# Half of each MLP down product as seven products for eight, woven with the next up chunk

## The chip, the cores and the metric

The kernel runs on one core of one Trainium2 chip. The metric is the time of one execution on the device in microseconds (us), as the median of three runs. A profile is one further execution, recorded by the hardware profiler; its span is shorter than a run's time by what lies around the program.

## The reference

A decoder trunk of two layers over 256 tokens of 2048 channels, all in float32. Each layer adds a mixer (layer 0: attention and pooling, layer 1: a gated convolution) and then an MLP whose hidden width is 8192. The change concerns the MLP:

```python
def _mlp(h, w_up, w_down):
    return jnp.square(jax.nn.relu(h @ w_up)) @ w_down

for layer in range(DEPTH):                      # DEPTH = 2
    h = _rmsnorm(x, mix_norm_g[layer])
    ...                                         # x = x + mixer(h)
    x = x + _mlp(_rmsnorm(x, mlp_norm_g[layer]), w_mlp_up[layer], w_mlp_down[layer])
```

x is 256 x 2048, an up weight 2048 x 8192, a down weight 8192 x 2048.

## The kernel before

**Precision.** Every float32 operand of a matmul is held as two parts in a rounded float32 format: hi, the leading twelve bits of each element (a cast on ScalarE, ACT, L124), and lo, the rest (a subtraction on VectorE, DVE, L125). A product is hi x hi + hi x lo + lo x hi. `slab` (L110) loads 1 MB of a weight into a raw buffer over the sync engine's queue and makes from it two pairs of hi and lo tiles, each 128 partitions x 1024 elements. There are three raw buffers, and six hi and six lo tiles.

**Up.** The hidden width is cut into 16 chunks of 512 columns. `up_chunk(c)` goes through `columns_chunk` (L153): four slabs, each with four blocks of 128 input channels (kt). For each kt and each of four column tiles, `columns_out` issues a matmul of 512 columns with the weight's hi (L144: the activations' hi and lo side by side) and one of 256 columns with its lo (L145). The results stand transposed (hidden columns in the partitions, tokens in the free axis) in two PSUM tiles of two banks each. There are four such tiles (`bank2`). `sum_halves` then adds the two halves of a result (ACT copies one to t, L171; DVE adds, L173), DVE makes relu squared in one instruction (L693), and `split` writes hi (ACT, L177) and lo (DVE, L178) into hT, which later serves as the stationary operand.

**Down.** A pair is two chunks, 1024 rows of the down weight. `down_block(pair, b)` makes 512 of the 2048 output columns for both blocks of 128 tokens: 2 slabs x 4 rows' tiles x 2 token blocks x 3 matmuls = 48 matmuls of 512 columns (`tokens_out`, L137, L138, L139), summed up in two PSUM banks. Two DVE instructions (L717) then scale these by the norm's 1/r^2 of each token and add them onto x.

**Order.** The loop at the end of `mlp` makes chunks 0 and 1 of a layer first. Then, for each of eight pairs, come an up chunk of the next pair, down blocks 0 and 1, the other up chunk, and down blocks 2 and 3. A half round is one up chunk and two down blocks, a round two of these. The program is written as one sequence. The framework's scheduler gives each engine its own sequence from it, with semaphores where an operand or a buffer has to be waited for. An engine works strictly in the order of its own sequence, and loads are issued by the sync engine (SP) in the same way, each when its raw buffer comes free.

## Time and profile before

| | before |
|---|---|
| time, median of 3 runs | 2065.22 us (2065.14 to 2070.14) |
| span of the profiled execution | 2063.8 us |
| matmuls that load a weight's lo or hi, up: L144 and L145 | 2816 each |
| matmuls for tokens: L137, L138, L139 | 1344 each |
| MB read from HBM | 380.39 |

Engines are PE (TensorE's matmuls), PEld (its weight loads, beside the matmuls), DVE (VectorE), ACT (ScalarE), POOL (GpSimd) and SP (SyncE). A row of a group reads: line, engine, operation, output <- inputs (partitions x elements), count | busy time, mean ns of one | idle time of the engine ahead of them, and what ended it. A row of a timeline starts with the start and the length in us and ends with the idle time ahead of it in brackets, if any. A row of the waits reads: the waiting instruction <- what released it: us, count, longest. The chain that ended last is followed back from the last instruction to what released each one. Of PE the recorded length of a matmul (0.39 us) overlaps the next one's, so its pace is read from the starts.

### The profile page before, as it was taken

What the parts mean: (1) busy time and instruction counts of PE and PEld (TensorE: products, weight loads), DVE (VectorE), ACT (ScalarE), POOL (GpSimd) and SP (SyncE); (2) the same over time, 40 slices, a digit from 0 to 9 for tenths busy, and PEclk for the clock granted to TensorE, in tenths of its full rate; (3) what the DMA queues carried; (4) which work ended last, traced back from release to release, by engine and by line L of the source; (5) the groups of instructions that cost most, each with busy time, mean ns of one, the idle gap of its engine ahead of it and who ended that gap; (6) DMA issues with size and microseconds to landing.
All of it is one profiled execution on the core that took longest, in us unless ns stands there. A gap on an engine that the chain in (4) does not pass through costs nothing.

```text
span 2063.8 us, 26221 instructions
## 1 busy us (share of the span) xinstructions
PE 2050.2 (99%) x10702; PEld 1751.5 (85%) x10702; DVE 1237.2 (60%) x1445; ACT 947.7 (46%) x1204; POOL 52.5 (3%) x76
## 2 busy tenths in 40 slices
PE   8999999999999999999999999999999999999999
PEld 7988888888888888888888888888888888888887
DVE  5677566555555555566666666556556555555554
ACT  5576554444444444444444444444444444444442
POOL 2330000000000000000000000000000000000000
PEclk9999999999999999999999999999999999999999
DMA  7553555555555555555555555555555555555553
GB/s 261 163 198 130 163 180 188 185 196 190 184 187 192 192 184 188 193 190 184 184 184 193 195 184 190 182 190 193 184 190 191 190 185 189 197 185 184 190 195 125
DMA packets 195817, 384.18 MB, mean 186 GB/s; under 512 B 6224, under 2 KB 16336, under 8 KB 195696
## 3 DMA queue, kind: packets, MB, share of 16 engines
q1 hardware_dynamic: 195312, 382.23, 56.5%
q8 instruction: 83, 1.36, 0.3%
q0 software_dynamic: 352, 0.27, 0.1%
q14 instruction: 38, 0.31, 0.0%
q10 hardware_dynamic: 32, 0.01, 0.0%
HBM read 380.39 MB, written 2.10 MB: 185 GB/s over the span
## 4 chain that ended last, share of the span: by engine, by line
PE 98%; DMA 1%; ACT 1%; SPq 0%; DVE 0%; issue 0%
PE ps L144 32%; PE ps L145 16%; PE ps L139 16%; PE ps L138 15%; PE ps L137 15%; PE ps L150 1%; PE ps L151 1%; PE ps L152 1%; PE ps L268 1%; DMA raw<-in_even_w_in 1%; PE ps L586 0%; PE ps L590 0%; ACT hi L124 0%; PE ps L578 0%; PE ps L622 0%; ACT junk L479 0%
## 5 line engine op out<-in xcount | busy, mean ns | idle before, releaser
L125 DVE TENSOR_TENSOR lo<-raw,hi 128x1024 fp32r<-128x1024 f32 (+2 forms) x722 | 884.3, 1226 | 704.9 <-ACT hi L124 704.0
L124 ACT CAST hi<-raw 128x1024 fp32r<-128x1024 f32 (+2 forms) x722 | 756.3, 1049 | 958.2 <-PE ps L144 497.1
L144 PE MATMUL ps<-xT,hi 128*128 128x512 f32 x2816 | 988.1, 396 | 0.0
L145 PE MATMUL ps<-xT,lo 128*128 128x256 f32 x2816 | 786.5, 279 | 0.0
L144 PEld LDWEIGHTS ps<-xT,hi 128*128 128x128 f32 x2816 | 528.5, 188 | 126.8
L145 PEld LDWEIGHTS ps<-xT,lo 128*128 128x128 f32 x2816 | 530.7, 188 | 1.2
L139 PE MATMUL ps<-hi,hT 128*128 128x512 f32 (+1 forms) x1344 | 526.7, 392 | 0.0
L137 PE MATMUL ps<-hi,hT 128*128 128x512 f32 (+1 forms) x1344 | 524.2, 390 | 0.0
L138 PE MATMUL ps<-lo,hT 128*128 128x512 f32 (+1 forms) x1344 | 523.7, 390 | 0.0
L138 PEld LDWEIGHTS ps<-lo,hT 128*128 128x128 f32 x1344 | 252.4, 188 | 55.2
L137 PEld LDWEIGHTS ps<-hi,hT 128*128 128x128 f32 x1344 | 252.4, 188 | 55.1 <-issue 1.3
L139 PEld LDWEIGHTS ps<-hi,hT 128*128 128x128 f32 x1344 | 252.5, 188 | 52.5
L717 DVE SCALAR_TENSOR_TENSOR x<-ps,r,x 128x512 f32<-128x512 f32 x129 | 90.5, 742 | 36.2 <-PE ps L139 36.1
L171 ACT COPY t<-ps 128x512 f32<-128x512 f32 x88 | 51.2, 582 | 50.9 <-PE ps L145 50.9
L173 DVE TENSOR_TENSOR h<-ps,t 128x512 f32<-128x512 f32 x64 | 43.9, 687 | 16.9 <-ACT t L171 16.9
L177 ACT CAST hT<-sq 128x512 fp32r<-128x512 f32 x64 | 39.8, 622 | 16.0 <-DVE sq L693 16.0
L693 DVE SCALAR_TENSOR_TENSOR sq<-h 128x512 f32<-128x512 f32 x64 | 44.3, 692 | 2.1
L178 DVE TENSOR_TENSOR hT<-sq,hT 128x512 fp32r<-128x512 f32 x64 | 43.8, 684 | 0.0
L181 ACT ACTIVATE xT<-ps,gains 128x256 fp32r<-128x256 f32 x64 | 30.1, 470 | 28.9 <-DVE xT L182 25.3
L137 PE MATMUL ps<-hi,xT 128*128 128x384 f32 (+1 forms) x96 | 32.8, 343 | 5.5 <-ACT hi L124 3.0
L182 DVE SCALAR_TENSOR_TENSOR xT<-ps,gains,xT 128x256 fp32r<-128x256 f32 x64 | 30.7, 480 | 12.4 <-ACT xT L181 12.2
L150 PE MATMUL ps<-xT,hi 128*128 128x256 f32 x128 | 36.4, 284 | 0.0
(157 smaller groups left out, 679.0 us busy)
## 6 DMA issues: line engine op xcount, KB each, us to landing
raw<-in_w_mlp_up SPq DMA_DIRECT2D x128, 1024.0 KB, 5.2
raw<-in_w_mlp_down SPq DMA_DIRECT2D x128, 1024.0 KB, 5.0
raw<-in_odd_w_in SPq DMA_DIRECT2D x48, 1024.0 KB, 5.1
raw<-in_even_w_out SPq DMA_DIRECT2D x16, 1024.0 KB, 5.1
raw<-in_odd_w_out SPq DMA_DIRECT2D x16, 1024.0 KB, 5.0
raw<-in_even_w_in SPq DMA_DIRECT2D x8, 1024.0 KB, 5.4
raw<-in_even_w_in SPq DMA_DIRECT2D x7, 1088.0 KB, 6.6
raw<-in_even_w_ukv SPq DMA_DIRECT2D x4, 1024.0 KB, 5.2
```

The source lines that it names most:

```text
L124: a = nc.scalar.copy(h, r)
L125: v = nc.vector.tensor_tensor(out=l, in0=r, in1=h.bitcast(F32), op=ALU.subtract)
L137: nc.tensor.matmul(o, lhsT=a_hi, rhs=hi[:, c0:c0 + n], start=first, stop=False)
L138: nc.tensor.matmul(o, lhsT=a_hi, rhs=lo[:, c0:c0 + n], start=False, stop=False)
L139: nc.tensor.matmul(o, lhsT=a_lo, rhs=hi[:, c0:c0 + n], start=False, stop=last)
L144: nc.tensor.matmul(o, lhsT=hi[:, c0:c0 + P], rhs=act[:, kt, :], start=first, stop=False)
L145: nc.tensor.matmul(o[:, S:2 * S], lhsT=lo[:, c0:c0 + P], rhs=act[:, kt, 0:S], start=False, stop=last)
L150: nc.tensor.matmul(o, lhsT=hi[:, c0:c0 + P], rhs=act[:, kt, 0:S], start=first, stop=False)
L171: nc.scalar.copy(t, ps[:, :, S:2 * S])
L173: nc.vector.tensor_tensor(out=u, in0=ps[:, :, 0:S], in1=t, op=ALU.add)
L693: nc.vector.scalar_tensor_tensor(out=sq, in0=u, scalar=0.0, in1=u, op0=ALU.max, op1=ALU.mult)
L717: nc.vector.scalar_tensor_tensor(out=xb, in0=ps[:, t, :n], scalar=r2[0][:, t:t + 1], in1=xb, op0=ALU.mult, op1=ALU.add)
```

## The change

For all pairs but the last of each layer, output columns 0 to 1023 (down blocks 0 and 1) are computed by `down_seven`. It takes the product as 2 x 2 x 2 blocks: two token blocks, even and odd tiles of rows, and two blocks of 512 columns. Instead of eight block products (96 matmuls in all) it makes seven, P1 to P7, of 12 matmuls each (L764 to L766), by an identity of the Strassen family. Some of the seven take sums of blocks as operands. Sums of weight blocks are made in place on DVE, four a pair of 128 x 2048 elements (L783, L786), ahead of the cut into hi and lo. Sums of the activations' blocks are made in `sum_forms` (L744, L745, L746, and a cut into hi and lo), behind each up result. The seven results are combined by further sums (L783), partly from copies that ACT keeps in SBUF (L779), and go onto x by L790.

The seven products are woven with up chunk 2p+2: P1, slab 0, P2, slab 1, P3, slab 2, P4, slab 3, P5, then that chunk's tail (its sums, relu, square and forms) together with P6 and P7. Then come up chunk 2p+3 and down blocks 2 and 3 as before. Relu squared is now two ACT instructions (L728, L730) in all chunks. The pools of raw buffers and halves are opened anew by `new_stage` for each stage of the program: two raw buffers in the MLP stage instead of three, with three block buffers of the same size beside them, and a place is waited for tile by tile. The last pair is computed as before.

The bodies of `slab` and `columns_chunk` are cut in two: `halved` makes hi and lo of a raw tile (casts at L140, subtractions at L141), and `columns_steps` stops behind each slab. The lines move: L144 and L145 are L160 and L161 now, L137 to L139 are L153 to L155, L171 and L173 are L194 and L196, L177 and L178 are L200 and L201, L717 is L850.

```diff
-    raws = ctx.enter_context(tc.tile_pool(name="raws", bufs=3))
-    halves = ctx.enter_context(tc.tile_pool(name="halves", bufs=6))
+    def new_stage(raw_bufs, **more):
+        for s_ in stage:
+            s_.close()
+        st = ExitStack()
+        stage[:] = [st]
+        pools.clear()
+        for name, bufs in dict(raws=raw_bufs, halves=6, **more).items():
+            pools[name] = st.enter_context(tc.tile_pool(name=uid(name), bufs=bufs, reuse_waits="tile"))
...
     def mlp(layer, ss, xT, after=None):
...
+        new_stage(2, blocks=3, forms=2)
+        pairs = DFF // NB // 2
         def up_chunk(c):
+            pss = []
+            yield from columns_steps(pss, up, xT, c * NB, 4)
             hT = act_tile()
-            for i, ps in enumerate(columns_chunk(up, xT, c * NB, 4)):
+            seven = c < 2 * (pairs - 1)
+            if seven:
+                fT = pools["forms"].tile([P, 2, 2, 4, P], F32R, tag="fT", name=uid("fT"))
+            for i, ps in enumerate(pss):
                 u = sum_halves(ps, "h")
+                nc.scalar.activation(u, u, AF.Relu)
                 sq = small.tile([P, 2, S], F32, tag="sq", name=uid("sq"))
-                nc.vector.scalar_tensor_tensor(out=sq, in0=u, scalar=0.0, in1=u, op0=ALU.max, op1=ALU.mult)
+                nc.scalar.activation(sq, u, AF.Square)
                 split(hT[:, 2 * i:2 * i + 2, 0:S], hT[:, 2 * i:2 * i + 2, S:2 * S], sq)
+                if seven:
+                    sum_forms(fT[:, i], sq.rearrange("p e (t s) -> p (e t) s", t=T))
...
+        def sum_forms(fT, a):
+            f = small.tile([P, 4, P], F32, tag="u", name=uid("f"))
+            nc.vector.tensor_tensor(out=f[:, 0:2, :], in0=a[:, 1:2, :].to_broadcast([P, 2, P]), in1=a[:, 0:4:3, :], op=ALU.subtract)
+            nc.vector.tensor_tensor(out=f[:, 2, :], in0=a[:, 3, :], in1=f[:, 0, :], op=ALU.subtract)
+            nc.vector.tensor_tensor(out=f[:, 3, :], in0=a[:, 2, :], in1=f[:, 2, :], op=ALU.subtract)
+            split(fT[:, 0], fT[:, 1], f)
+        def down_seven(pair):
...
+            def product(o, b, left):
+                for q, (hi, lo) in enumerate(halved(b)):
+                    a_hi, a_lo = left(2 * pair + q // 2, q % 2)
+                    nc.tensor.matmul(o, lhsT=a_hi, rhs=hi, start=q == 0, stop=False)
+                    nc.tensor.matmul(o, lhsT=a_hi, rhs=lo, start=False, stop=False)
+                    nc.tensor.matmul(o, lhsT=a_lo, rhs=hi, start=False, stop=q == 3)
...
+            yield
+            b11 = block(0, 0)
+            one = bank2()
+            product(one[:, 0, :], b11, own(0, 0))
+            s1 = kept(one[:, 0, :])
+            yield
+            b12 = block(0, 1)
+            minus(b11, b12, b11)
+            product(one[:, 1, :], b11, form(1))
+            s5 = kept(one[:, 1, :])
+            onto(0, 0, s1)
+            yield
+            b22 = block(1, 1)
+            two = bank2()
+            product(two[:, 0, :], b22, form(3))
+            onto(0, 1, two[:, 0, :])
+            yield
+            plus(b12, b22, b12)
+            plus(b22, b22, b11)
+            product(two[:, 1, :], b22, form(2))
+            plus(s1, two[:, 1, :], s1)
+            yield
+            three = bank2()
+            product(three[:, 0, :], b12, form(0))
+            e = pools["forms"].tile([P, NB], F32, tag="part", name=uid("part"), bufs=3)
+            plus(e, three[:, 0, :], s1)
+            onto(1, 0, e)
+            plus(s1, s1, s5)
+            onto(0, 1, s1)
+            plus(s5, e, s5)
+            onto(1, 1, s5)
+            yield
+            b21 = block(1, 0)
+            product(three[:, 1, :], b21, own(0, 1))
+            onto(0, 0, three[:, 1, :])
+            yield
+            minus(b22, b21, b22)
+            four = bank2()
+            product(four[:, 0, :], b22, own(1, 1))
+            onto(1, 0, four[:, 0, :])
...
+        for p in range(pairs - 1):
+            products, slabs = down_seven(p), up_chunk(2 * p + 2)
+            next(products)
+            for at in range(5):
+                next(products)
+                if at < 4:
+                    next(slabs)
+            whole(slabs)
+            whole(products)
+            whole(up_chunk(2 * p + 3))
+            for b in (2, 3):
+                down_block(p, b, False)
+        for b in range(4):
+            down_block(pairs - 1, b, True)
```

The first place is DVE's sequence where a half round ends and the next up chunk begins. Before the change (raw1004 is the first slab of that up chunk, ps979 and ps990 are the results of the two down blocks ahead of it):

```order
L125 TENSOR_TENSOR lo1000_6348<-raw996_6341,hi999_6347 128x1024
L125 TENSOR_TENSOR lo1006_6383<-raw1004_6380,hi1005_6382 128x1024
L717 SCALAR_TENSOR_TENSOR x_76<-ps979_6235,r2459_2894,x_76 128x512 x2
L125 TENSOR_TENSOR lo1008_6387<-raw1004_6380,hi1007_6386 128x1024
L125 TENSOR_TENSOR lo1011_6425<-raw1009_6422,hi1010_6424 128x1024
L125 TENSOR_TENSOR lo1013_6429<-raw1009_6422,hi1012_6428 128x1024
L125 TENSOR_TENSOR lo1016_6467<-raw1014_6464,hi1015_6466 128x1024
L717 SCALAR_TENSOR_TENSOR x_76<-ps990_6306,r2459_2894,x_76 128x512 x2
```

The first lo of the up chunk, lo1006, stands ahead of the additions onto x of both down blocks.

With the change DVE has, between the product P5 and the up chunk that follows P6 and P7 (the first bank of ps1175 is P5's, the second P6's, ps1196 is P7's; part tiles are the kept results, f the sums of activations, raw1203 the up chunk's first slab):

```order
L141 TENSOR_TENSOR lo1200_7087<-b1155_6866,hi1199_7086 128x1024
L744 TENSOR_TENSOR f1186_7036<-sq1185_7032 128x256
L783 TENSOR_TENSOR part1180_7018<-ps1175_6997,part1136_6752 128x512
L745 TENSOR_TENSOR f1186_7036<-sq1185_7032,f1186_7036 128x128
L790 SCALAR_TENSOR_TENSOR x_79<-part1180_7018,r2470_2931,x_79 128x512
L783 TENSOR_TENSOR part1136_6752<-part1136_6752,part1149_6821 128x512
L201 TENSOR_TENSOR hT1181_7025<-sq1185_7032,hT1181_7025 128x2x256
L790 SCALAR_TENSOR_TENSOR x_79<-part1136_6752,r2470_2931,x_79 128x512
L783 TENSOR_TENSOR part1149_6821<-part1180_7018,part1149_6821 128x512
L746 TENSOR_TENSOR f1186_7036<-sq1185_7032,f1186_7036 128x128
```

These are the last lo of P7, the sums that follow P5, and the forms of the up chunk's first result. They are followed without a gap by:

```order
L790 SCALAR_TENSOR_TENSOR x_79<-part1149_6821,r2470_2931,x_79 128x512
L196 TENSOR_TENSOR h1188_7044<-ps1138_6755,t1187_7042 128x512
L201 TENSOR_TENSOR fT1182_7026<-f1186_7036,fT1182_7026 128x512
L790 SCALAR_TENSOR_TENSOR x_79<-ps1175_6997,r2470_2931,x_79 128x512
L790 SCALAR_TENSOR_TENSOR x_79<-ps1196_7081,r2470_2931,x_79 128x512
L201 TENSOR_TENSOR hT1181_7025<-sq1189_7047,hT1181_7025 128x2x256
L744 TENSOR_TENSOR f1190_7051<-sq1189_7047 128x256
L141 TENSOR_TENSOR lo1205_7108<-raw1203_7105,hi1204_7107 128x1024
L745 TENSOR_TENSOR f1190_7051<-sq1189_7047,f1190_7051 128x128
L141 TENSOR_TENSOR lo1207_7112<-raw1203_7105,hi1206_7111 128x1024
```

The first lo of the next up chunk, lo1205, now stands behind all additions onto x of the seven products and behind most of the tail of the chunk before.

The second place is the same boundary in PE's sequence. Before, the last matmuls of a down block and the first of the up chunk:

```order
L137 MATMUL ps990_6306<-hi999_6347,hT848_5390 128x512
L138 MATMUL ps990_6306<-lo1000_6348,hT848_5390 128x512
L139 MATMUL ps990_6306<-hi999_6347,hT848_5390 128x512
L144 MATMUL ps1002_6378<-xT370_2325,hi1005_6382 128x512
L145 MATMUL ps1002_6378<-xT370_2325,lo1006_6383 128x256
```

The second matmul of the up chunk is the first to take its lo. With the change, from the last matmuls of P7:

```order
L764 MATMUL ps1196_7081<-hi1199_7086,hT1098_6555 128x512
L765 MATMUL ps1196_7081<-lo1200_7087,hT1098_6555 128x512
L766 MATMUL ps1196_7081<-hi1199_7086,hT1098_6555 128x512
L160 MATMUL ps1201_7103<-xT374_2333,hi1204_7107 128x512
L160 MATMUL ps1202_7104<-xT374_2333,hi1204_7107 128x512
L161 MATMUL ps1201_7103<-xT374_2333,lo1205_7108 128x256
```

The scheduler has put two matmuls with hi (one for each of the two results) ahead of the first with lo; the three rows above them end the seven products.

## The prediction

> **What bounds the kernel now.** I read the page first, then the waits of PE, then the rounds of the MLP in the timelines.

> ```profile
> span 2063.8 us, 26221 instructions
> PE 2050.2 (99%) x10702; PEld 1751.5 (85%) x10702; DVE 1237.2 (60%) x1445; ACT 947.7 (46%) x1204; POOL 52.5 (3%) x76
> PE 98%; DMA 1%; ACT 1%; SPq 0%; DVE 0%; issue 0%
> ```

> The chain that ended last is PE for 98%. PE's waits show where it was ever held:

> ```profile
> PE ps L209 <- DMA rows<-in_mix_norm_g: 3.4, 1, 3.4
> PE ps L137 <- ACT hi L124: 3.0, 1, 3.0
> PE ps L137 <- ACT xT L181: 2.6, 1, 2.6
> ```

> These are the three longest, all in the first 20 us; in the MLP there are none. So the kernel is as long as its matmuls: a matmul removed counts in full, as long as PE gets no new wait. A stretch of the MLP shows what is spare on the other engines (the columns are PE, PEld, DVE, ACT, POOL busy, then the clock):

> ```profile
> 500.00:582.00 82.00, 82.00 (x415) 69.24 (x415) 46.96 (x48) 35.67 (x38) 0.00 (x0) 1.00 0.58 189
> ```

> DVE has 35 of 82 us free, ACT 46. The pitch of the two kinds of matmul, and the length of a half round (one up chunk and two down blocks), come from starts in the timelines:

> ```profile
> 573.72 0.39 PE L138 MATMUL ps<-lo,hT 128*128 128x512 f32 x1
> ...
> 576.93 0.39 PE L137 MATMUL ps<-hi,hT 128*128 128x512 f32 x1
> ...
> 555.72 0.40 PE L144 MATMUL ps<-xT,hi 128*128 128x512 f32 x1
> ...
> 557.13 0.40 PE L144 MATMUL ps<-xT,hi 128*128 128x512 f32 x1
> ...
> 564.05 0.59 ACT L171 COPY t<-ps 128x512 f32<-128x512 f32 x1 [1.19 <-PE ps L145]
> ...
> 608.64 0.59 ACT L171 COPY t<-ps 128x512 f32<-128x512 f32 x1 [1.19 <-PE ps L145]
> ```

> Down matmuls start 3.21 us / 14 = 0.229 us apart. An up pair (L144 and L145) takes 1.41 / 4 = 0.353. A half round is 44.59 us, a pair of chunks 89.18.

> **What the change removes.** In 14 pairs (7 in each layer) the down blocks 0 and 1 had 2 x 48 = 96 matmuls; seven products of 12 are 84. 14 x 12 = 168 fewer at 0.229 is **38.5 us**, certain as far as PE keeps its pitch. A pair then needs 89.18 - 2.75 = 86.43 us of PE.

> **What it adds, on DVE.** Its durations, by form:

> ```profile
> L125 DVE TENSOR_TENSOR lo<-raw,hi 128x1024 fp32r<-128x1024 f32 x704 | 863.7, 1228 | 689.9 <-ACT hi L124 689.1
> L124 ACT CAST hi<-raw 128x1024 fp32r<-128x1024 f32 x704 | 738.9, 1051 | 946.0 <-PE ps L144 497.1 <-PE ps L139 430.9 <-issue 13.7
> L717 DVE SCALAR_TENSOR_TENSOR x<-ps,r,x 128x512 f32<-128x512 f32 x127 | 89.5, 746 | 32.0 <-PE ps L139 31.9
> L171 ACT COPY t<-ps 128x512 f32<-128x512 f32 x88 | 51.2, 582 | 50.9 <-PE ps L145 50.9
> L693 DVE SCALAR_TENSOR_TENSOR sq<-h 128x512 f32<-128x512 f32 x64 | 44.3, 692 | 2.1
> L173 DVE TENSOR_TENSOR h<-ps,t 128x512 f32<-128x512 f32 x64 | 43.9, 687 | 16.9 <-ACT t L171 16.9
> L178 DVE TENSOR_TENSOR hT<-sq,hT 128x512 fp32r<-128x512 f32 x64 | 43.8, 684 | 0.0
> L177 ACT CAST hT<-sq 128x512 fp32r<-128x512 f32 x64 | 39.8, 622 | 16.0 <-DVE sq L693 16.0
> L260 ACT ACTIVATE junk<-x 128x512 f32<-128x512 f32 x32 | 20.2, 631 | 0.7 <-DVE x L643 0.2
> L472 DVE TENSOR_TENSOR turned<-qkv,other 128x64 f32<-128x64 f32 x16 | 2.9, 221 | 0.1
> ```

> A tensor_tensor costs 0.687 at 512 columns and 1.228 at 1024, so about 2.31 at 2048 (same slope, an estimate; bounds 2.2 and twice 1.228 = 2.46); between 0.221 at 64 and 0.687 at 512, 0.42 at 256 and 0.29 at 128. Per pair DVE now has 38 lo (46.7), 4 sums of weight blocks (9.2), 12 h, hT and fT (8.2), 12 for the forms (4.0), 4 sums of products (2.7) and 11 additions onto x (7.9): 78.7 us, where it had 32 lo (39.3), 12 h, sq and hT (8.3) and 8 onto x (6.0), 53.6. That is 91% of PE's 86.43. Not yet a bound, but DVE takes its queue in order, so what counts is what stands ahead of the operand that PE wants next.

> In the woven part (P1 U0 P2 U1 P3 U2 P4 U3 P5: five products of 12 x 0.229 = 2.75 and four slabs of 16 x 0.353 = 5.65) PE needs 36.35 us. DVE's queue in that stretch holds 17 lo, 2 weight sums, 4 onto x, a sum, an h and a form: 30 us. I count no stall there: by the same queue each lo is ready 4.9 us or more before PE wants it (tightest at U3's first half). It could cost up to 1 us a pair if a weight sum were 0.3 us dearer than its upper bound.

> **Where the queue jams.** Behind P5, PE has only P6 and P7, then wants the first lo of the next up chunk. In DVE's queue that lo is the sixteenth instruction from the + that reads P5's bank, so none of the sixteen can start before P5 ends. How closely DVE's instructions follow each other:

> ```profile
> 564.66 0.69 DVE L173 TENSOR_TENSOR h<-ps,t 128x512 f32<-128x512 f32 x1 [0.55 <-ACT t L171]
> 565.39 0.69 DVE L693 SCALAR_TENSOR_TENSOR sq<-h 128x512 f32<-128x512 f32 x1
> 566.00 1.22 DVE L125 TENSOR_TENSOR lo<-raw,hi 128x1024 fp32r<-128x1024 f32 x1
> 567.13 0.69 DVE L178 TENSOR_TENSOR hT<-sq,hT 128x512 fp32r<-128x512 f32 x1
> 567.74 0.68 DVE L173 TENSOR_TENSOR h<-ps,t 128x512 f32<-128x512 f32 x1
> ```

> An independent follower starts 0.08 us before the end recorded for its forerunner (0.69 after 0.61), one that reads its forerunner's result 0.04 after it. The sixteen: four of 0.687 (three sums, one h), three of 0.684 (hT, fT, hT), three onto x from SBUF at 0.692 (as L693), two onto x from PSUM at 0.746, forms of 0.29, 0.29 and 0.42, and the lo of 1.228: 10.6 us, less 15 x 0.08 = 9.4. The + starts about 0.5 us after P5's end, since the form ahead of it needs a Square that ACT reaches late: hi for P7's second half gets its buffer when U3 ends, 2.75 before P5's end, and 1.05 + relu 0.62 + t 0.58 + Square 0.63 follow. Another 0.1 goes at the second hT, which waits for relu, Square and cast in a row. So the lo is done 10.0 us after P5's end. PE meanwhile does 24 matmuls (5.50) and the two hi matmuls that need no lo (0.46): it stands for **4.0 us**. Bounds: no late start and no wait of ACT, 3.4; no overlap between neighbours, 5.3. I take 4.0, nearest to the rows. In the six pairs of a layer whose next chunks are cut into forms the queue is the same: 12 x 4.0 = **48 us**. In the seventh, the lo stands ahead (second lo at about 9.2, wanted at 8.7): 2 x 0.5 = 1 us. In a layer's first pair the tail of chunk 1 falls into the woven part and P1's second half waits for it, 1 us each: 2.

> **The rest.** On ACT 6 casts hi (6.3), relu and Square (5.0), 4 fT (2.5) and 2 copies (1.2) more per pair bring 38 us to 53 of 86: hidden beside the matmuls, except where named; if the cover were gone PE would wait as for DVE. On SP:

> ```profile
> raw<-in_w_mlp_up SPq DMA_DIRECT2D x128, 1024.0 KB, 5.2
> ```

> The number and size of loads stay; four of a pair's eight down loads are now blocks. Two raw buffers are freed at worst every 5.6 us, a load takes 5.2 and six halves are held ahead: nothing, at worst 5.2 us once in a stage. At the start of the convolution the second slab's load must wait for the MLP's last matmul (its place was a halves buffer): 5.2 + 1.05 + 1.23 = 7.5 against 5.65 + 0.87 of transposes + 0.23 on PE: 0.7 us. For all stage changes 0 to 5; I take 0.7.

> Without more: 2063.8 - 38.5 + 48 + 1 + 2 + 0.7 = 2077.0.

> **What the stall does to PE's clock.** PE's matmuls around the one wait that came after the clock had once been full, and the windows behind it (the clock is the last number but two):

> ```profile
> 16.88 0.31 PE L139 MATMUL ps<-hi,xT 128*128 128x320 f32 x1
> 19.75 0.44 PE L137 MATMUL ps<-hi,xT 128*128 128x384 f32 x1 [2.57 <-ACT xT L181]
> ...
> 20.00:21.00 1.00, 1.00 (x5) 0.77 (x4) 1.00 (x2) 0.47 (x1) 0.00 (x0) 0.70 1.02 403
> 22.00:23.00 1.00, 1.00 (x5) 1.00 (x6) 0.57 (x1) 1.00 (x2) 0.00 (x0) 0.50 0.88 254
> 23.00:24.00 1.00, 1.00 (x6) 1.00 (x6) 1.00 (x2) 0.50 (x2) 0.00 (x0) 0.59 0.83 252
> 24.00:25.00 1.00, 1.00 (x8) 1.00 (x7) 1.00 (x2) 0.36 (x1) 0.00 (x0) 1.00 1.01 418
> ```

> After 2.57 idle us the clock is half from 20.4 (0.70 is 0.4 us at full) to 23.8 (0.59 is 0.18 at full): 3.4 us at half, 1.7 lost. If it is judged in periods of 3.4 us that run on by themselves, a gap of 4.0 leaves one period with 2.57 idle us in two cases of three, and one with 2.0 always. So 8 to 12 of the 12 stalls lose 1.7: 14 to 20 us, I take 16. 2077.0 + 16 = 2093 of span. [...]

> The span is that of one profiled execution; the runs shown have a median of 2065.22, 1.4 more, which lies around it. So **2095 us**.

> **Rivals.** (a) The stall comes, the clock holds: 2077.0 + 1.4 = 2078. For it: that drop was among the kernel's first matmuls, and two hi matmuls may break the gap. (b) The tail is hidden, and it gets faster. One mechanism: the sixteen are through when P7 ends, so PE never stands; 2063.8 - 38.5 + 3.7 + 1.4 = 2030. It decides below 3.2 us a stall (38.5 / 12). For it: DVE is free for 7.7 us a pair by the sums; against: the + can't start before P5's end, and even 15 followers at their closest leave 3.4. (c) The gain and the stalls cancel: stalls of 2.5 to 3.5 us without the clock, 2060 to 2072. (d) DVE is the bound in the woven part too: were a weight sum 2.3 us dearer (read and written in place by a busy engine), three of them stand ahead of U3's first lo and eat its 4.9 us: 2 us in 14 pairs, 28 more, 2106 to 2123. Against: no row shows an SBUF instruction slowed. That the change does not cut the matmuls can't be: they are 168 fewer in the order.

> **How the numbers follow.** Forecast with the clock, 2088 to 2104: 0.52. (a) 0.22. (b) 0.10. (c) 0.10. (d) 0.06. No change that a measurement of this kernel could tell is within 0.3%, 2059 to 2071.4. So faster 0.10, the same 0.11 (c, and (a) at a stall of 3.4), slower 0.79. The range of 8 in 10 takes in the forecast, (a) and most of (c), 2063 to 2108; (b) and (d) are left out.

> **What would show it.** A PE wait at the first lo of an up chunk (its L161), 12 times, near 4 us, released by DVE; none inside the woven part; windows behind it at a clock near 0.5; DVE near 90% busy in the MLP; 7 x 12 product matmuls in a pair at 0.229. Wrong it would be if that wait were under 3.2 us, if the clock stayed at 1.00, or if PE waited for weight sums between P1 and P5.

## The result, and the profile after

| | before | changed |
|---|---|---|
| time, median | 2067.68 us (2065.14 to 2071.89, 4 runs) | 2116.36 us (2115.18 to 2120.35, 4 runs) |
| ratio to before | | 1.0243, 95% interval 1.0230 to 1.0255 |
| span of the profiled execution | 2063.8 us | 2113.7 us |

The change made the kernel slower, as forecast, but by 48.7 us instead of 30, and outside the range that ended at 2108. The page of the changed kernel first, the chain of the work that ended last, and then PE's longest waits:

```profile
span 2113.7 us, 26545 instructions
PE 2047.5 (97%) x10534; PEld 1745.7 (83%) x10534; DVE 1535.1 (73%) x1843; ACT 1126.1 (53%) x1500; POOL 52.5 (2%) x76
PE 88%; DVE 6%; ACT 3%; issue 1%; POOL 1%; DMA 1%; SPq 0%; ACTq 0%; DVEq 0%; POOLq 0%
```

```profile
PE ps L161 <- DVE lo L141: 43.5, 13, 3.6
PE ps L238 <- DMA rows<-in_mix_norm_g: 3.6, 1, 3.6
PE ps L160 <- ACT hi L140: 3.2, 1, 3.2
PE ps L166 <- ACT qkv L521: 2.5, 1, 2.5
PE ps L153 <- ACT xT L204: 2.2, 1, 2.2
PE ps L153 <- ACT hi L140: 2.0, 1, 2.0
PE ps L166 <- ACT hi L140: 1.9, 1, 1.9
```

PE is no longer the whole chain: DVE has 6% of it. There is a wait in the MLP now, at the first lo of an up chunk: 12 times 3.61 us; the thirteenth wait of that row, 0.2 us, is at the convolution's start. The timeline of DVE at the first of the twelve (P6 and P7 are 24 matmuls, so P5 ends at about 370.03 - 24 x 0.228 = 364.55), and below it PE's timeline:

```profile
362.96 1.22 DVE L141 TENSOR_TENSOR lo<-b,hi 128x1024 fp32r<-128x1024 f32 x1 [0.41 <-ACT hi L140]
364.50 0.43 DVE L744 TENSOR_TENSOR f<-sq 128x256 f32<-128x256 f32 x1 [0.31 <-ACT sq L730]
364.84 0.68 DVE L783 TENSOR_TENSOR part<-ps,part 128x512 f32<-128x512 f32 x1
365.44 0.28 DVE L745 TENSOR_TENSOR f<-sq,f 128x128 f32<-128x128 f32 x1
365.64 0.74 DVE L790 SCALAR_TENSOR_TENSOR x<-part,r,x 128x512 f32<-128x512 f32 x1
...
370.86 1.41 DVE L790 SCALAR_TENSOR_TENSOR x<-ps,r,x 128x512 f32<-128x512 f32 x2
372.33 0.69 DVE L201 TENSOR_TENSOR hT<-sq,hT 128x512 fp32r<-128x512 f32 x1
372.94 0.42 DVE L744 TENSOR_TENSOR f<-sq 128x256 f32<-128x256 f32 x1
373.27 1.22 DVE L141 TENSOR_TENSOR lo<-raw,hi 128x1024 fp32r<-128x1024 f32 x1
```

```profile
370.03 0.90 PE L160 MATMUL ps<-xT,hi 128*128 128x512 f32 x2
374.55 0.38 PE L161 MATMUL ps<-xT,lo 128*128 128x256 f32 x1 [3.61 <-DVE lo L141]
```

From the sum that reads P5 (364.84) to the end of the lo (374.49) DVE has no row with idle time: these are the sixteen instructions of the prediction. PE goes from 370.03 to 374.55, 4.52 us, with two matmuls (0.46), so the wait costs about 4.07 us. The idle time shown, 3.61, is smaller because the record of a matmul runs on past its pace (0.90 us for these two, where two take 0.46 by the pace).

Behind each of the twelve waits the clock falls to 0.50. The windows at the second of the twelve (PE waits until 465.90):

```profile
463.00:464.00 1.00, 0.00 (x0) 0.00 (x0) 0.92 (x2) 0.62 (x1) 0.00 (x0) 1.00 0.00 0
464.00:465.00 1.00, 0.00 (x0) 0.00 (x0) 1.00 (x3) 0.00 (x0) 0.00 (x0) 0.69 0.00 0
465.00:466.00 1.00, 0.10 (x1) 0.10 (x1) 1.00 (x3) 0.00 (x0) 0.00 (x0) 0.50 0.00 0
...
470.00:471.00 1.00, 1.00 (x5) 0.81 (x5) 0.26 (x1) 0.00 (x0) 0.00 (x0) 0.50 1.02 385
471.00:472.00 1.00, 1.00 (x6) 0.89 (x6) 0.00 (x0) 0.00 (x0) 0.00 (x0) 0.89 1.01 350
```

0.69 means that the half clock begins at 464.38, 0.89 that it ends at 471.22: 6.84 us, of which 1.52 are still in the wait, so 5.32 / 2 = 2.66 us are lost, if half the clock counts as half the pace. By the starts it is a little less: the up pairs (L160 and L161) start every 0.640 us from 466.28 to 470.97 and every 0.349 behind 471.22, so 5.32 x (1 - 0.349 / 0.640) = 2.42. Counted at half, seven of the twelve waits are followed by 6.8 us at half (2.44 to 2.66 lost, 18.0 together), five by 3.4 us (1.45 to 1.70 lost, 8.2 together).

The account by terms, in us of span (2113.7 - 2063.8 = 49.9):

| term | forecast | found |
|---|---|---|
| 168 matmuls fewer | -38.5 | -38.5 (count as forecast) |
| 12 waits at the first lo | 48 | 12 x 4.07 = 48.8 |
| seventh pair, first pairs | 3 | 0.2 |
| half clock behind the 12 waits, counted at half | 16 | 26.3 |
| stage changes | 0.7 | 12.3 |
| the rest | 0 | 0.8 |

The 12.3 are: the first up matmul of layer 0 at 280.44 instead of 274.61 (5.8, mostly a wait of 1.94 at 68 us and one of 2.48 at 160 us in the mixer, each followed by 3.4 us at half clock), the wait of 3.25 at the convolution's start and 1.6 of half clock behind it, and 1.6 at the transposes that stand in each MLP's first matmuls.

The rest of 0.8 is small only because two things cancel. From the first up matmul of one stage to that of the next, the two MLPs are 37.8 us longer in sum than before, 3.9 less than the terms that fall there, and the convolution is 6.3 longer, 4.5 more than its terms. Of the 3.9, 2.4 are the half clock, which comes to 23.9 instead of 26.3 by the pace of 0.640; the others are the pace of matmuls that wait for nothing (last section).

### The profile page after: what moved, and what is told of

The parts are those of the page before. It is cut to its first block, busy times and chain, and to the rows that moved or that the text cites. A ratio compares the mean times of both kernels' runs of the same rounds, so it can differ in the third digit from the quotient of the medians.

```text
span 2113.7 us, 26545 instructions
## 1 busy us (share of the span) xinstructions
PE 2047.5 (97%) x10534; PEld 1745.7 (83%) x10534; DVE 1535.1 (73%) x1843; ACT 1126.1 (53%) x1500; POOL 52.5 (2%) x76
## 4 chain that ended last, share of the span: by engine, by line
PE 88%; DVE 6%; ACT 3%; issue 1%; POOL 1%; DMA 1%; SPq 0%; ACTq 0%; DVEq 0%; POOLq 0%
PE ps L160 31%; PE ps L161 16%; PE ps L153 10%; PE ps L155 10%; PE ps L154 10%; PE ps L764 3%; PE ps L766 3%; PE ps L765 3%; DVE lo L141 1%; DVE x L790 1%; DVE part L783 1%; ACT hi L140 1%; DVE hT L201 1%; ACT sq L730 1%; ACT h L728 1%
## 5 line engine op out<-in xcount | busy, mean ns | idle before, releaser
L160 PE MATMUL ps<-xT,hi 128*128 128x512 f32 x2816 | 1016.6, 402 | 3.8 <-ACT hi L140 3.2
L141 DVE TENSOR_TENSOR lo<-raw,hi 128x1024 fp32r<-128x1024 f32 (+2 forms) x610 | 735.9, 1225 | 334.6 <-ACT hi L140 333.1
L140 ACT CAST hi<-raw 128x1024 fp32r<-128x1024 f32 (+2 forms) x610 | 629.3, 1048 | 506.6 <-PE ps L160 141.8
L161 PE MATMUL ps<-xT,lo 128*128 128x256 f32 x2816 | 802.6, 286 | 43.7 <-DVE lo L141 43.5
L160 PEld LDWEIGHTS ps<-xT,hi 128*128 128x128 f32 x2816 | 540.7, 192 | 134.6 <-PE ps L766 5.4
L161 PEld LDWEIGHTS ps<-xT,lo 128*128 128x128 f32 x2816 | 542.0, 192 | 53.7 <-DVE lo L141 49.5
L153 PE MATMUL ps<-hi,hT 128*128 128x512 f32 (+1 forms) x896 | 349.2, 390 | 0.0
L155 PE MATMUL ps<-hi,hT 128*128 128x512 f32 (+1 forms) x896 | 347.5, 388 | 0.0
L154 PE MATMUL ps<-lo,hT 128*128 128x512 f32 (+1 forms) x896 | 347.0, 387 | 0.0
L140 ACT CAST hi<-b 128x1024 fp32r<-128x1024 f32 x196 | 206.0, 1053 | 219.1 <-PE ps L160 118.8
L141 DVE TENSOR_TENSOR lo<-b,hi 128x1024 fp32r<-128x1024 f32 x196 | 238.5, 1220 | 76.2 <-ACT hi L140 76.1
L153 PEld LDWEIGHTS ps<-hi,hT 128*128 128x128 f32 x896 | 168.3, 188 | 35.1 <-issue 1.3
L155 PEld LDWEIGHTS ps<-hi,hT 128*128 128x128 f32 x896 | 168.2, 188 | 34.9
L154 PEld LDWEIGHTS ps<-lo,hT 128*128 128x128 f32 x896 | 168.3, 188 | 33.4
L194 ACT COPY t<-ps 128x512 f32<-128x512 f32 x88 | 50.8, 580 | 70.9 <-PE ps L161 70.9
L764 PE MATMUL ps<-hi,fT 128*128 128x512 f32 x224 | 88.4, 394 | 0.0
L766 PE MATMUL ps<-hi,fT 128*128 128x512 f32 x224 | 87.7, 392 | 0.0
L765 PE MATMUL ps<-lo,fT 128*128 128x512 f32 x224 | 87.1, 389 | 0.0
L196 DVE TENSOR_TENSOR h<-ps,t 128x512 f32<-128x512 f32 x64 | 43.7, 686 | 34.1 <-ACT t L194 34.1
L764 PE MATMUL ps<-hi,hT 128*128 128x512 f32 x168 | 65.8, 393 | 0.2 <-ACT hT L200 0.2
L786 DVE TENSOR_TENSOR b<-b,b 128x2048 f32<-128x2048 f32 x28 | 64.0, 2287 | 2.7 <-DMA b<-in_w_mlp_down 2.2
## 6 DMA issues: line engine op xcount, KB each, us to landing
raw<-in_w_mlp_up SPq DMA_DIRECT2D x128, 1024.0 KB, 5.3
raw<-in_w_mlp_down SPq DMA_DIRECT2D x72, 1024.0 KB, 5.2
b<-in_w_mlp_down SPq DMA_DIRECT2D x56, 1024.0 KB, 6.0
raw<-in_odd_w_in SPq DMA_DIRECT2D x48, 1024.0 KB, 5.2
raw<-in_even_w_out SPq DMA_DIRECT2D x16, 1024.0 KB, 5.2
raw<-in_odd_w_out SPq DMA_DIRECT2D x16, 1024.0 KB, 5.3
raw<-in_even_w_in SPq DMA_DIRECT2D x8, 1024.0 KB, 5.6
```

The lines of the kernel that those rows point to most:

```text
L140: a = nc.scalar.copy(h, r)
L141: v = nc.vector.tensor_tensor(out=l, in0=r, in1=h.bitcast(F32), op=ALU.subtract)
L153: nc.tensor.matmul(o, lhsT=a_hi, rhs=hi[:, c0:c0 + n], start=first, stop=False)
L154: nc.tensor.matmul(o, lhsT=a_hi, rhs=lo[:, c0:c0 + n], start=False, stop=False)
L155: nc.tensor.matmul(o, lhsT=a_lo, rhs=hi[:, c0:c0 + n], start=False, stop=last)
L160: nc.tensor.matmul(o, lhsT=hi[:, c0:c0 + P], rhs=act[:, kt, :], start=first, stop=False)
```

## The experiments

Theory **J**, the jam: the first lo is late only through what stands ahead of it in DVE's queue. Its rival **L**, the load: DVE has too much to do in a woven pair, and the wait would come back elsewhere. A third question is the clock, a fourth the stages. A diff here is against the changed kernel, if nothing else is said. Ratios are to the kernel before. Where an edit adds lines, the line numbers of that run's views are one or more higher: in c1_spread, c6_conv and c9_conv_both L161 is the up matmul with hi and L162 that with lo.

**c1_spread.** `later` is a list, from which each slab of the next up chunk takes one entry behind its matmuls.

```diff
-            plus(e, three[:, 0, :], s1)
-            onto(1, 0, e)
-            plus(s1, s1, s5)
-            onto(0, 1, s1)
-            plus(s5, e, s5)
-            onto(1, 1, s5)
+            later.append(lambda: (plus(e, three[:, 0, :], s1), onto(1, 0, e)))
+            later.append(lambda: (plus(s1, s1, s5), onto(0, 1, s1)))
+            later.append(lambda: (plus(s5, e, s5), onto(1, 1, s5)))
...
-            onto(0, 0, three[:, 1, :])
...
-            onto(1, 0, four[:, 0, :])
+            later.insert(0, lambda: (onto(0, 0, three[:, 1, :]), onto(1, 0, four[:, 0, :])))
```

> The sums and additions onto x that follow P5, P6 and P7 (eight DVE instructions a pair) are issued two at a time behind the four slabs of the next up chunk instead of ahead of them. Theory J (the jam: the first lo of the up chunk is late only because of what stands ahead of it in DVE's queue): the 12 waits of 3.61 us (43.3) go, and with them the half clock behind them (26.3): 2116.4 - 69.6 = 2047 us, 2042 to 2052. Rival L (DVE has too much work in the woven pairs, and the wait only shows at that place): waits of about the same sum come back at later slabs, 2105 to 2120.

2038.63 us, ratio to before 0.9867 (0.9851 to 0.9884): 1.3% faster than the kernel before, and 8 us better than J's figure, below its range. Of the 8 us, 5.5 are an error in that figure: it took the idle time shown (43.3) for what the waits cost (48.8). Its longest waits of PE, and a whole pair, from the first up matmul behind P7 on (the columns are those of the prediction's windows); the last row is a pair of the changed kernel, from the end of one wait to the end of the next:

```profile
PE ps L241 <- DMA rows<-in_mix_norm_g: 3.5, 1, 3.5
PE ps L161 <- ACT hi L141: 3.2, 1, 3.2
PE ps L167 <- ACT qkv L524: 2.7, 1, 2.7
...
369.10:455.10 86.00, 86.00 (x440) 73.23 (x439) 73.92 (x84) 50.87 (x61) 0.00 (x0) 1.00 0.62 197
```

```profile
374.55:465.90 91.35, 87.69 (x437) 74.01 (x437) 73.49 (x82) 50.82 (x60) 0.00 (x0) 0.97 0.57 185
```

No wait for DVE's lo is left, PE is busy for all of the 86 us, and the clock is full. DVE does the same work as in the changed kernel (73.92 and 73.49 us). L falls: with the same load the waits are gone.

**c2_block.** The same eight instructions, all behind the first slab.

```diff
+            def tail():
+                plus(e, three[:, 0, :], s1)
+                onto(1, 0, e)
...
+            waiting.append(tail)
...
-            onto(0, 0, three[:, 1, :])
+            waiting.append(lambda: onto(0, 0, three[:, 1, :]))
...
-            onto(1, 0, four[:, 0, :])
+            waiting.append(lambda: onto(1, 0, four[:, 0, :]))
```

> The same eight instructions, all behind the first slab of the next up chunk. J: the first lo is in time, but now 14 instructions (8.9 us with a lo of 1.2 at their end) stand between the first slab's second lo and the second slab's first lo, which I reckon 13.4 us after P5's end where PE wants it at 11.4: 12 waits of about 2 us, at the second slab; with the clock halved behind some seven of them about 2085 us (2050 to 2100). L: the same sum of waits as in the changed kernel, 2105 to 2120.

2061.04 us, 0.9972 (0.9960 to 0.9983).

```profile
PE ps L161 <- DVE lo L141: 17.4, 12, 1.5
```

The jam has moved to where the queue said, the second slab: 12 waits, of 1.44 to 1.50 us shown and 1.6 by the starts, instead of 2. No half clock follows any of them, where I had expected it behind some seven.

**c3_two.** Only the last two of the edits of c2_block, those for P6 and P7.

> Only the additions onto x of P6 and P7 are put behind the first slab; the first lo is then twelfth instead of sixteenth behind the sum that reads P5. J: each wait is shorter by two additions, a cut and a form, 2.3 us: 12 waits of 1.3. Clock: if it is judged by windows of 3.4 us in which some 1.7 idle us are needed, no stretch at half follows, and the time is 2116.4 - 27.6 - 26.3 = 2062 us; if the loss of clock went with the idle time, 9.5 us of it would stay, 2072. L: 2105 to 2120.

2059.86 us, 0.9965 (0.9951 to 0.9980).

```profile
PE ps L161 <- DVE lo L141: 14.7, 13, 1.2
...
455.41 0.91 PE L160 MATMUL ps<-xT,hi 128*128 128x512 f32 x2
457.51 0.39 PE L161 MATMUL ps<-xT,lo 128*128 128x256 f32 x1 [1.19 <-DVE lo L141]
...
460.00:470.00 10.00, 10.00 (x58) 8.69 (x58) 6.50 (x7) 3.25 (x4) 0.00 (x0) 1.00 0.71 218
```

2.10 - 0.46 = 1.64 us a wait, 2.43 less than the 4.07 of the changed kernel, where the queue's count gave 2.3. The clock stays full in the MLPs, and the time is that of the first case, 2062 and not 2072: the loss of clock did not shrink in proportion to the idle time, it went.

**c4_no_sums.** Leaves out the four sums of weight blocks of each pair; what it computes is then another result.

```diff
-            minus(b11, b12, b11)
...
-            plus(b12, b22, b12)
-            plus(b22, b22, b11)
...
-            minus(b22, b21, b22)
```

> Leaves out the four sums of weight blocks of each pair (the products take the blocks as loaded), 9.2 us of DVE a pair; everything else stays. J: none of the four stands between the sum that reads P5 and the first lo, so the 12 waits stay 3.6 us and the time 2114 to 2118. L: DVE is at 80% instead of 90%, and the waits shrink or go: 2047 to 2090.

2118.39 us, 1.0248 (1.0232 to 1.0263), the same as the changed kernel's 1.0243.

```profile
PE ps L161 <- DVE lo L141: 43.6, 13, 3.6
```

About 9 us of DVE's work a pair taken away change nothing, since they do not stand in the queue between P5 and the lo. That is the second way in which L falls.

**c5_pools.** The kernel before with the new pools: the changed kernel with the loop and the relu squared of before, and three raw buffers in the MLP. It also keeps the change's other edits of buffers (the squares' scratch tile shares the buffers of t, and the mixer's constants lie in a pool of their own), so it tests these together.

```diff
-        new_stage(2, blocks=3, forms=2)
+        new_stage(3)
...
-            seven = c < 2 * (pairs - 1)
+            seven = False
...
+            for half in range(2):
+                if not last:
+                    whole(up_chunk(2 * p + 2 + half))
+                for b in (2 * half, 2 * half + 1):
+                    down_block(p, b, last)
```

> The kernel before with the new pools alone: raw buffers and halves are opened anew at each stage (three raw buffers in the MLP), the MLP computed as before, without the seven products and with relu squared on DVE. Theory S (the opening of stages costs time by itself): the waits ahead of the MLP (5.8 us with their clock) and at the convolution's start (3.3, and 1.6 to 3 of clock) are there, 2066.6 + 8 to 14 = 2075 to 2081 us, and the rounds keep their length. Rival: these waits came with the seven products' loads and order, and this is 2066 to 2068.

2069.41 us, 1.0014 (1.0005 to 1.0023): neither theory's figure.

```profile
PE ps L166 <- ACT qkv L521: 2.6, 1, 2.6
PE ps L166 <- ACT hi L140: 1.9, 1, 1.9
```

The waits ahead of the MLP are there, and its first up matmul starts at 279.00, 4.4 us later than before: these do come with the buffers. The 1.4 us that are missing to 5.8 are near the 1.7 that a stretch of 3.4 us at half clock is counted with, so I take it that one such stretch less came here; that is an estimate. At the first of the two waits (1.9) ACT's first two casts (67.02) stand behind six copies of a result; before, one cast was done ahead of these, at 63.57. No wait stands at the convolution's start, so that one does not come with the buffers alone. And the stages' lengths, from the starts of their first up matmuls, changed with no wait to show for it: both MLPs together are 7.5 us shorter, the convolution is 6.0 us longer.

**c6_conv.** Against c1_spread: the wait at the convolution's start. ACT had the last squares of the MLP's result ahead of the convolution's first two casts, and these squares waited for DVE's last additions onto x. In the changed kernel:

```profile
1014.78 0.63 ACT L289 ACTIVATE junk<-x 128x512 f32<-128x512 f32 x1 [2.78 <-DVE x L850]
...
1016.07 1.97 ACT L140 CAST hi<-raw 128x1024 fp32r<-128x1024 f32 x2
...
1017.15 1.07 PE L160 MATMUL ps<-xT,hi 128*128 128x512 f32 x2 [3.25 <-ACT hi L140]
```

```diff
             turn_block(xT, b, which, i)
-            squares(ss, b)
+            with behind(*last_prep[:1] if which == "mix1" and b == 3 else ()):
+                squares(ss, b)
```

> c1_spread with one edit more: ACT's last two squares of the MLP's result are put behind the first slab's two casts for the convolution, which stood behind them in ACT's queue. Theory Q (the wait of 3.25 us at the convolution's start is a queue order again, not the place in memory): it falls to 0.7 at most and 1.6 to 3 us of half clock go with it: 2038.6 - 5.5 = 2033 us, 2031 to 2036. Rival (the cast waits for its place, which the MLP's last matmul frees): no change, 2037 to 2040.

2035.84 us, 0.9851 (0.9838 to 0.9865); its interval overlaps that of c1_spread. The timelines of ACT, DVE and PE at the start of the convolution:

```profile
971.78 1.99 ACT L141 CAST hi<-raw 128x1024 fp32r<-128x1024 f32 x2
...
973.83 1.41 DVE L850 SCALAR_TENSOR_TENSOR x<-ps,r,x 128x512 f32<-128x512 f32 x2 [1.42 <-PE ps L156]
975.15 2.35 DVE L142 TENSOR_TENSOR lo<-raw,hi 128x1024 fp32r<-128x1024 f32 x2
...
976.42 0.38 PE L162 MATMUL ps<-xT,lo 128*128 128x256 f32 x1 [2.17 <-DVE lo L142]
```

The casts now run ahead of the MLP's end, so their place in memory was not what they waited for. But the lo has the same trouble on DVE: two additions onto x stand ahead of it. The wait shrank from 3.25 to 2.17, not to 0.7 at most as theory Q had it.

**c7_relu_dve.** Relu squared on DVE again.

```diff
-                nc.scalar.activation(u, u, AF.Relu)
...
-                nc.scalar.activation(sq, u, AF.Square)
+                nc.vector.scalar_tensor_tensor(out=sq, in0=u, scalar=0.0, in1=u, op0=ALU.max, op1=ALU.mult)
```

> The changed kernel with relu squared as one DVE instruction, as before, instead of two on ACT. J: the first lo is nineteenth instead of sixteenth behind the sum that reads P5 (a square and three forms more, a cut less, +0.75 us), while the wait for ACT's late Square (0.5) goes: waits of 3.9 us, 12 x 0.3 = 4 more, about 2120 us (2114 to 2128). Rival (ACT's two instructions are what holds up the tail): waits of 3.1, about 2109.

2134.22 us, 1.0336 (1.0320 to 1.0352), above my range.

```profile
PE ps L161 <- DVE lo L141: 62.1, 15, 4.8
...
464.52 0.63 PE L160 MATMUL ps<-xT,hi 128*128 128x512 f32 x2
469.92 0.58 PE L161 MATMUL ps<-xT,lo 128*128 128x256 f32 x1 [4.78 <-DVE lo L141]
```

The wait costs 5.40 - 0.46 = 4.94 us, 0.87 more; the queue's count gave 0.75, and the gain of 0.5 that I set against it did not come. Two waits of 2.33, in the seventh pairs, come on top. Relu squared on ACT is a part of the change that pays.

**c8_no_weave.** The seven products in one piece.

```diff
-            next(products)
-            for at in range(5):
-                next(products)
-                if at < 4:
-                    next(slabs)
-            whole(slabs)
-            whole(products)
+            whole(products)
+            whole(slabs)
```

> The changed kernel with the seven products in one piece ahead of the up chunk instead of woven with it. From P1's start DVE has 14 lo, three sums of weight blocks and 12 sums and additions of products, about 30 us, for 19.25 us of PE work: waits of 8 to 10 us a pair, in pieces, for 43.3 us of waits at the chunk's first lo that go. 2116 + 70 to 100, with the clock about 2215 us (2170 to 2260). Rival (the weave does nothing, DVE is prepared ahead): the 12 waits go and none come, 2047 to 2075.

2166.10 us, 1.0479 (1.0465 to 1.0493), below my range.

```profile
PE ps L764 <- DVE part L783: 39.4, 14, 3.5
PE ps L764 <- ACT hi L140: 18.7, 12, 2.3
PE ps L765 <- DVE lo L141: 10.5, 16, 1.1
```

The waits at the up chunk's first lo are gone; some 69 us come in these three groups, about 5 us a pair instead of 8 to 10. The weave does hide DVE's work, and what it left uncovered was the tail.

**c9_conv_both.** Against c6_conv: the additions, too, are put behind.

```diff
+                if last and layer == 0 and b == 3:
+                    def add_late(add=add):
+                        with behind(*last_prep):
+                            add()
+                    waiting.append(add_late)
+                else:
+                    add()
```

> c6_conv with one edit more: the two additions onto x of the MLP's last down block (1.41 us) are put behind the first slab's two lo for the convolution, which stood behind them in DVE's queue. Q (queue order on both engines): the wait of 2.17 us that c6_conv still has there goes, and 1.7 of half clock with it: 2035.8 - 3.9 = 2032 us, 2030 to 2034. Rival (the place in memory, or the wait moves to the second slab, whose load is still under way): a wait of 2 to 3 us stays within the first slabs, 2035 to 2037.

2033.69 us, 0.9841 (0.9827 to 0.9854), the lowest median here: 1.6% under the kernel before.

```profile
PE ps L162 <- DVE lo L142: 0.6, 1, 0.6
```

At the convolution's first slab there is no wait; one of 0.61 remains at its second. That one is the load: it was issued at 974.28, behind the MLP's last matmul, and ACT's casts waited for it until 979.35. From c1_spread to here it is 4.9 us in the medians, but the intervals overlap by a little, and the profiled spans differ by 1.5 us only, since the convolution's pace was slower in the later one (last section). So the waits show what the two edits do, and the time shows it weakly.

## Why the prediction was wrong

**The gain and the jam were right.** The order of the queue gave the place, the count of twelve and the price: 4.0 us forecast, 4.07 found; the lo was to be done 10.0 us after P5's end and is done 9.9 after it (374.49 - 364.55). Two small misses cancel in this: the sum starts 0.3 us after P5's end and not 0.5, and the sixteen take 9.65 us (364.84 to 374.49) and not 9.5. The runs bear out that it is the queue: the price goes with what stands between the sum that reads P5 and the lo.

| kernel | place of the first lo behind that sum | cost of a wait, us | ratio to before |
|---|---|---|---|
| c3_two | twelfth | 1.64 | 0.9965 |
| changed | sixteenth | 4.07 | 1.0243 |
| c7_relu_dve | nineteenth | 4.94 | 1.0336 |
| c1_spread | ahead of it | 0 | 0.9867 |

**The term of the clock was mis-sized.** "8 to 12 of the 12 stalls lose 1.7: 14 to 20 us, I take 16" failed in two ways: all twelve lost something, and seven lost a second period, since the wait ran on into it: 1.51 to 1.94 us of that period were idle in the seven, 0.52 at most in the other five. It came to 26.3 us instead of 16. The step that said so was "a gap of 4.0 leaves one period with 2.57 idle us in two cases of three, and one with 2.0 always": 2.57 was the only case in the trace, and I took it for the point from which the clock falls. In the changed kernel 1.67 idle us in the period ahead sufficed (the wait from 831.35, with the half clock from 833.02). That wait was cut by the boundary and left 1.67 us ahead of it and 1.94 behind, and both periods were followed by one at half; the prediction counted one period a stall. The equal periods that the prediction assumed are seen in the changed kernel: its half stretches behind the twelve waits last 3.41 or 6.83 us, and those of the second to sixth wait begin 92.16 us apart, 27 x 3.413, and end likewise.

**The stage changes were the other miss.** "For all stage changes 0 to 5; I take 0.7": found 12.3. I looked at the load of the second slab at the convolution's start, and not at ACT's and DVE's queues there, where c6_conv and c9_conv_both show the cause: casts behind squares, and lo behind additions onto x. It is the jam again, at a place where I did not read the order. The 0.7 itself is borne out: in c9_conv_both, where nothing hides it, the second slab's wait is 0.61. For the mixer the prediction had no term, although the pools are opened anew there too. Of its 5.8 us, 4.4 come with the new buffers (c5_pools); which of these edits makes each wait was not tried.

**Too high**: 1 for the seventh pair and 2 for the first pairs; 0.2 was found. DVE's share came out lower as well: 73.5 us a pair (73.9 in c1_spread) and not 78.7, since the sum of the recorded lengths counts the overlap of neighbours (0.08 us in the prediction's rows) twice.

With 26.3 and 12.3 for 16 and 0.7 the forecast would have been 2117. Rival (a), the clock holds, is refuted for waits of this length and true for those of c2_block and c3_two. Rival (b), the tail is hidden, is what c1_spread makes true. Rival (d), in whose range the time came to lie by accident, did not happen: PE's waits show none in the woven part but one of 0.22, and a weight sum takes 2.29 us, within its bounds (a group of the changed kernel's page):

```profile
L786 DVE TENSOR_TENSOR b<-b,b 128x2048 f32<-128x2048 f32 x28 | 64.0, 2287 | 2.7 <-DMA b<-in_w_mlp_down 2.2
```

## What to carry to other kernels

Look for the operand that the busiest engine wants next, and count what stands ahead of it in the queue that makes it and cannot start before a late event: here this decided, not the load (2116.36 us and 2038.63 in c1_spread, with 73.5 and 73.9 us of DVE a pair). Work that nobody waits for (a sum onto a result, a square for a norm) goes behind the next stage's first operands, and spread out rather than in a block (2038.63 us in c1_spread, 2061.04 in c2_block). A wait of PE cost its length here. In the changed kernel the waits shown with 3.6 us cost 1.45 to 2.66 us more through the clock, counted at half; in c2_block and c3_two those of 1.2 to 1.5 us cost nothing more.

## What was not expected of the hardware

Matmuls that waited for nothing did not always keep one pace. The convolution's windows, before and in the changed kernel:

```profile
989.88:1347.81 357.93, 357.93 (x1956) 308.58 (x1955) 221.15 (x264) 163.90 (x193) 1.31 (x7) 1.00 0.57 187
```

```profile
1017.15:1381.35 364.20, 364.01 (x1955) 313.07 (x1955) 218.34 (x256) 162.39 (x189) 0.81 (x7) 1.00 0.57 187
```

These are the same matmuls, 6.3 us longer, of which 1.6 are the half clock at the start and 0.2 a wait. The pairs of up matmuls start every 0.347 us there before, every 0.353 in the changed kernel, every 0.354 in c9_conv_both, and every 0.349 in c1_spread. In the MLPs it is 0.347 in the first four chunks before and 0.353 in the others; in the changed kernel it is 0.349, and 0.353 for stretches behind some of the waits. c5_pools, whose matmuls are those of the kernel before, has 0.349 in the MLPs and 0.354 in the convolution. So the pace took one of a few values in these runs (0.347, 0.349, 0.353 to 0.354) and kept it for long stretches. What sets it was not tried and stays open; it is 4 to 6 us of a stage.
